# Filter spectra of a hybrid diffusion backbone on one Trainium2 core: stacked fp32r features, mirrored taps folded into sums and differences, one table for all slots

## The chip, the core and the metric

The kernel is one program on one core of a Trainium2 chip. The metric is device microseconds of that core from launch to end. Three timed runs of the kernel before gave 3165.01, 3173.91 and 3177.1 us; their median, 3173.91 us, is the time before.

The core's engines run side by side, each through its own queue in order: PE (matrix products), DVE (VectorE), ACT (ScalarE), POOL (GpSimd), and SP, which only issues DMAs. An engine waits for another through semaphores; whatever stands behind a waiting instruction on the same engine waits too.

## What is computed

The reference is a two-layer backbone over 2048 tokens of width 1024 (with 256 context tokens). Layer 0 is a pooling mixer beside attention with 6 query heads; layer 1 is a long-convolution mixer beside a Fourier mixer. The part that matters here are the filters of the long convolutions, which depend on no token: a small network gives 64 features for each of 2048 lags, a matrix turns them into taps for 768 channels, 2 orders and 2 directions, and the taps are damped and normalized.

```python
hdn = jnp.sin(fr * (hdn @ w2.astype(f32) + b2.astype(f32)))
h = (hdn @ w3.astype(f32)).reshape(L, HY_ORDER, 2, HY_WIDTH)
...
h = h * decay[:, None, None, :]
h = h / (jnp.sum(jnp.abs(h), axis=(0, 2), keepdims=True) + EPS)
zero = jnp.zeros((1, HY_ORDER, HY_WIDTH), f32)
return jnp.concatenate([h[:, :, 0], zero, h[:0:-1, :, 1]], axis=0)
...
kf = jnp.fft.rfft(kfull, n=2 * L, axis=0)
return jnp.fft.irfft(zf * kf[None], n=2 * L, axis=1)[:, :L]
```

The kernel stores `kf`, the spectra of 12 filters (6 blocks of 128 channels, 2 orders), and uses them in layer 1.

## The kernel before

The program has four stretches by the trace: layer 0's projections (0 to about 590 us), layer 0's attention (597 to 1755 us), a short stretch with layer 0's output projection, and layer 1 (from 2075 us on). **All of the change but a few instructions lies in the attention stretch**, because the spectra are computed in between the attention's matrix products.

*Attention.* There are 96 blocks of 128 queries (`blocks`). For each, PE computes five tiles of scores `S` in three products each (L306 to L308, fp32r in two parts), DVE takes maxima `mx` (L1295), ACT the exponentials into `pb` (L1306), PE transposes `pb` into `pt` (L1317), ACT and DVE split it into two parts `ph` and `pl` (L300, L303), and PE multiplies these with the values into `o` (L1329 to L1333). `S` and `pt` share six PSUM banks. The order of all this is written out by hand in the four strings of `BLOCK`: `S`, `M`, `E`, `T`, `V`, `D`, `N` and `Z` stand for the steps, a capital `F` calls `fill()`, which takes the filters' generator one `yield` further, and a `p` takes the generator `weights()` (called `prep`) one `yield` further. Two blocks hold five `F`, six `p`, and at every eighth pair one more fill (`f`).

*Filters.* `filters()` (L1116) runs over 12 units. A unit takes eight groups `grp` of four slots (a slot holds the 128 lags of one residue modulo 16); a group takes two `yield`s and the last one two more, so that a unit takes 18 fills. In a group, PE makes four products of 64 features by 128 channels in fp32 into `hacc` (L1173); DVE multiplies by the damping into `ht` (L1174), makes negated copies `hn` of half of it (L1175), sums absolute values (L1178) and adds them to `rd` (L1181); PE takes the first factor of the 2048-lag transform with a table of its own for each slot, `fdft`, eight fp32 products into `fa` (L1200, L1201); ACT copies `fa` to the slots of `fX` (L1203). The PSUM pool of `hacc` and `fa` has one bank, which they take in turns. The last group also forms the norm (`smacc`).

Once the eight groups of a unit are there, the second factor, a 16-point transform over the slots, runs on POOL: `fft16` returns 44 POOL operations for 64 channels, twice a unit, and `some(FFT_N)`, called after most `yield`s, gives POOL the next six of them, then stores the finished tile to DRAM (`spec`, L1134) `FFT_LATE` calls later.

*Weights.* Beside this, `weights()` prepares later weights in pieces. For 23 pieces of layer 1's input projection: load `wraw`, cast it to `wodd` on ACT (L1381), subtract on POOL (L1383), two `p` later store `wodd`. For 32 pieces of the output projections a product by the gate on POOL (L1403) stands between load and cast. There is one buffer of `wodd`.

So POOL's queue holds transforms and weights in the order in which the program gives them, ACT's holds exponentials, splits, copies of `fa` and casts of `wodd`, and SP's all loads and stores.

Of the kernel before, what the change touches and what calls it, by code (L numbers as in the profile page):

```python
# [40 lines left out]

BLOCK = [
# [15 lines left out]
def constants():  # L58
    """Tables that depend on the shapes alone."""
# [30 lines left out]
    sel = [[2 * q + 1, (2 * q + 2) % 16, 15 - 2 * q, 14 - 2 * q] for q in range(8)]  # L90
    out["decay"] = np.stack([dec[:, :, q, :] for q in sel], 1)
# [26 lines left out]
def sbc(ap, n):  # L118
    """[p, f] -> [p, n, f], the same f for each n."""
    return ap.unsqueeze(1).to_broadcast([ap.shape[0], n, ap.shape[1]])  # L120


def lbc(ap, n):
    """[p, f] -> [p, f, n], each element n times."""
    return ap.unsqueeze(2).to_broadcast([ap.shape[0], ap.shape[1], n])


def fft16(v, X, T, inv, s=None):
    """16-point transforms over the slots of X[p, re/im, 16, C]; T is of the same shape.

    Forward takes slot 4a+b and leaves index k'+4k'' in slot 4k'+k''; inverse undoes it,
    without the factor 1/16. The operations come as a list, each with its us. With s, that engine does the products by constants, beforehand.
    """
# [6 lines left out]
    def at(A, start, *dims):  # L140
        """slots of A, as (stride, count) from start on"""
# [14 lines left out]
    def stt(out, in0, scalar, op, in1):  # L156
        """in0 already has its factor where s does the products, but for the sign"""
# [28 lines left out]
    def tan(n, *dims):  # L186
        """the slots from n on, times the tangent"""
# [16 lines left out]
    # the second four: slots k * e + b * o for b; 11 and 14 have the other sign  # L204
# [35 lines left out]
def tile_net(ctx, tc, i, k, out, keep=None):  # L240
# [33 lines left out]
    def y1_part(kk):  # L274
        """the place of gated channels of layer 1"""
# [6 lines left out]
    hdd = dram("hdd", (8, 64, 4, P))  # L282
# [30 lines left out]
    class Lane:  # L313
        """pieces for one engine, each of so many us, the next one at least so many later, or after an event"""
# [30 lines left out]
    class Jobs:  # L345
        """the order in which work is given to the engines: matrix products in front, the rest when they are that far"""
# [37 lines left out]
        def until(self, done):  # L384
            """let time pass until done()"""
# [15 lines left out]
    def load_wout(sp, wp, w, kks, dst, gb, wait=4.0, eng=sy, ve=v):  # L401
        """output projection times the gate, in two parts, one tile of rows at a time"""
# [21 lines left out]
    def load_gate(wp, n):  # L424
        """the gate of layer n, the same in every partition"""
# [4 lines left out]
    def rstd_steps(sp, ss, n, tag, scale):  # L430
        """ss [p, n] sums of squares -> 1 / sqrt(ss * scale + eps), with a Newton step after the square root"""
# [13 lines left out]
    def normed_steps(sp, xs):  # L445
        """each slab [p, D] of xs -> each row over its root mean square, in place"""
# [13 lines left out]
    def modulated_steps(sp, pp, xs, gs, sh, emit, lo_eng):  # L460
        """transposed, scaled and shifted, in two parts: emit(m) gives their places"""
# [12 lines left out]
    LASTE, LASTR, GATE2, FOLD1, HALF, SUM0, SUM1, ADDF, FEW, LASTW, IN_C, FFT_N, FFT_LATE, HL, DR, DE, EW0, EW1, SPLIT, SUMMED, QSEL, CV0, CV1, CV2, CV3, COL, NW0, NW1, FIRST_Z, MORE, X0_SQ, X0_STEP, TRAIL, C_EARLY, A_TURN, A_SLOW, A_AHEAD, A_W, A_PACE, LAG0, FOLD, WAIT, AHEAD, LAG, APART, LOW, W_LOAD, W_HIGH, W_LOW, ADDED, SLOW = 0, 0.5, 5, 6, 1.5, 0.2, 1.5, 3, 9, 3.5, 25, 6, 4, 3, 4, 4, 8.0, 2.5, 15, 0.5, 1, 14, 12, 8, 15, 5, 24, 0, 20.0, 8, [7, 7, 11, 11], (0, 0, 0, 0, 2, 2, 2, 2), 11, 1, 2.5, 0.25, 3.5, 4, 1.05, 7, 2, 6.0, 2.5, 5, 5, 2, 6, 6, 4, 8, 1.02  # L474
    # tokens in the order n2 * 128 + n1 for token 16 * n1 + n2
# [8 lines left out]
    def load_columns(raw, gi, kk, half, eng=sy):  # L484
        """128 rows of half of the columns of a group"""
# [1886 lines left out]
```

## Time and profile before

| what | value |
|---|---|
| median of three runs | 3173.91 us (3165.01 to 3177.1) |
| span of the profiled execution | 3162.6 us |
| its time around the span | not in the profile; the fastest timed run is 2.4 us above the span |
| attention stretch | 597 to 1755 us |
| filters' products in it (`hacc`, `fa`) | from 611 to 1651 us |
| granted TensorE clock in it | 1.00 from 659 us on |
| PE busy over the span | 2996.1 us (95%) |

The profile is read here by stretches: busy time of an engine in a stretch of known work, then the rows of single operations by their shape, then the waits. Matmul records overlap their neighbours, so what a matmul costs its queue is the distance from its start to the next one's, not its length.

### The profile page before, as it was taken

The page shows a single profiled execution, that of the slowest core. Times are in us where ns is not written, and L with a number is a line of the kernel's source. Part 1 is how long each engine was busy: PE and PEld are TensorE (multiplying, and loading weights), DVE is VectorE, ACT ScalarE, POOL GpSimd, SP SyncE. Part 2 cuts the span into 40 slices and gives each one's busy share as a digit, 9 for nine tenths or more (in the row PEclk, how much of TensorE's full clock was granted, in tenths as well). Part 3 has the DMA queues.
Part 4 walks back from the last instruction along what each step waited for, and adds up shares of the span by engine and source line. Part 5 has one row for each costly group of instructions (what it writes and reads, how often), then busy time and mean ns, then how long its engine had stood idle before and what let it go on. Part 6 is the DMA issues. An engine that isn't in the chain of part 4 may idle for free. (4 is left out here: it accounts for less than half of the span.)

```text
span 3162.6 us, 49927 instructions
## 1 busy us (share of the span) xinstructions
PE 2996.1 (95%) x18121; PEld 2589.2 (82%) x18121; DVE 2183.2 (69%) x4124; ACT 1329.8 (42%) x3130; POOL 1215.5 (38%) x1595
## 2 busy tenths in 40 slices
PE   8999999799999999999999999999989999988799
PEld 4888888699999998999898778777878787874587
DVE  4775437477777777777776443377789797978556
ACT  4444545355555555555556332322323232232123
POOL 3122223027888887878886344001010100101110
PEclk9999999899999999999999999999999999999899
DMA  6466345534444445444443777678899989976875
GB/s 223 157 202 202 125 132 162 182 107 127 121 140 132 128 127 169 121 125 133 117 115 117 250 261 256 242 258 283 275 290 288 293 282 314 275 260 167 233 210 176
DMA packets 425393, 614.72 MB, mean 194 GB/s; under 512 B 140278, under 2 KB 278200, under 8 KB 416698
## 3 DMA queue, kind: packets, MB, share of 16 engines
q1 hardware_dynamic: 399994, 528.43, 51.0%
q0 software_dynamic: 25152, 83.10, 11.2%
q8 instruction: 143, 2.34, 0.3%
q14 instruction: 104, 0.85, 0.1%
HBM read 388.60 MB, written 187.18 MB: 182 GB/s over the span
## 5 line engine op out<-in xcount | busy, mean ns | idle before, releaser
L303 DVE TENSOR_TENSOR pl<-pt,ph 128x512 fp32r<-128x512 f32 (+1 forms) x480 | 299.8, 633 | 137.1 <-ACT ph L300 136.1
L151 DVE TENSOR_TENSOR gB<-gB 128x256 f32<-128x256 f32 (+3 forms) x442 | 351.6, 845 | 51.2 <-ACT gB L1879 47.3
L300 ACT CAST ph<-pt 128x512 fp32r<-128x512 f32 (+1 forms) x480 | 253.5, 556 | 244.7 <-PE pt L1317 242.3
L306 PE MATMUL dacc<-dh,dw 128*128 128x512 f32 x768 | 312.2, 407 | 40.2 <-DMA dh<-h1T 39.5
L1306 ACT ACTIVATE pb<-S,mx 128x512 f32<-128x512 f32 (+1 forms) x480 | 309.7, 656 | 82.7 <-DVE mx L1298 59.4
L307 PE MATMUL dacc<-dh,dw 128*128 128x512 f32 x768 | 304.7, 397 | 0.0
L308 PE MATMUL dacc<-dh,dw 128*128 128x512 f32 x768 | 304.6, 397 | 0.0
L1295 DVE TENSOR_REDUCE mx<-S 128x1 f32<-128x512 f32 (+1 forms) x480 | 279.9, 629 | 18.6 <-DMA kh<-kT0h 14.0
L303 POOL TENSOR_TENSOR wl<-raw,wh 128x256 fp32r<-128x256 f32 x160 | 135.6, 880 | 368.6 <-ACT wh L300 356.7
L1317 PE MATMUL pt<-ident,pb 128*128 128x128 f32 x1728 | 248.0, 275 | 11.2 <-ACT pb L1306 10.9
L151 POOL TENSOR_TENSOR fX<-fT 128x128 f32<-128x128 f32 (+2 forms) x336 | 246.7, 757 | 4.9
L1329 PE MATMUL o<-ph,vh 128*128 128x256 f32 x864 | 233.0, 301 | 1.4 <-ACT ph L300 1.2
L151 POOL TENSOR_TENSOR fT<-fX 128x1024 f32<-128x1024 f32 (+1 forms) x192 | 202.6, 1081 | 49.0 <-ACT fX L1203 44.6
L1317 PEld LDWEIGHTS pt<-ident,pb 128*128 128x128 f32 x1728 | 197.2, 141 | 28.2 <-ACT pb L1306 14.8
L1330 PE MATMUL o<-ph,vl 128*128 128x256 f32 x864 | 216.5, 282 | 1.5 <-DMA vl<-vl 1.5
L306 PEld LDWEIGHTS dacc<-dh,dw 128*128 128x128 f32 x768 | 147.9, 193 | 78.2 <-DMA dh<-h1T 46.7
L306 PE MATMUL S<-kh,qh 128*128 128x512 f32 (+1 forms) x480 | 196.9, 410 | 9.9 <-DMA kl<-kT0l 8.2
L306 PE MATMUL acc<-wh,hh 128*128 128x256 f32 x672 | 197.2, 293 | 3.5 <-ACT qraw L969 2.4
L308 PE MATMUL acc<-wh,hl 128*128 128x256 f32 x672 | 193.1, 287 | 1.2 <-DVE hl L303 0.9
L307 PE MATMUL acc<-wl,hh 128*128 128x256 f32 x672 | 192.8, 287 | 0.9 <-POOL wl L303 0.8
L307 PE MATMUL S<-kl,qh 128*128 128x512 f32 (+1 forms) x480 | 180.4, 376 | 1.1 <-DMA kl<-kT0l 1.0
L308 PE MATMUL S<-kh,ql 128*128 128x512 f32 (+1 forms) x480 | 180.4, 376 | 0.0
(473 smaller groups left out, 7776.5 us busy)
## 6 DMA issues: line engine op xcount, KB each, us to landing
dh<-h1T SPq DMA_DIRECT2D x172, 512.0 KB
dec<-cst_decay_dram SPq DMA_DIRECT2D x96, 256.0 KB
spec<-fX SPq DMA_DIRECT2D x24, 1024.0 KB
dw<-wi SPq DMA_DIRECT2D x48, 512.0 KB
gK<-spec SPq DMA_DIRECT2D x48, 512.0 KB
raw<-in_ev_w_in_dram SPq DMA_DIRECT2D x160, 128.0 KB
u<-dev SPq DMA_DIRECT2D x70, 256.0 KB
cu<-u POOLq DMA_DIRECT2D x17, 1024.0 KB, 8.3
```

What stands on the lines that cost most here:

```text
L151: put(out, lambda: v.tensor_tensor(out=out, in0=in0, in1=in1, op=op))
L300: s.copy(hi, src)
L303: lo_eng.tensor_sub(lo, src, hi.bitcast(F32))
L306: pe.matmul(acc, ah, bh, start=first, stop=False)
L307: pe.matmul(acc, ah, bl, start=False, stop=False)
L308: pe.matmul(acc, al, bh, start=False, stop=last)
L1295: v.tensor_reduce(out=B["mx"][:, c : c + 1], in_=S[:, :n], axis=AX.X, op=ALU.max)
L1306: s.activation(B["pb"][:, c * 512 : c * 512 + n], B["S"][c][:, :n], AF.Exp, bias=B["mx"][:, 5:6], accum_out=B["sm"][:, c : c + 1])
L1317: pe.transpose(pt[:, t, :], B["pb"][:, (4 * c + t) * P : (4 * c + t + 1) * P], ident)
L1329: pe.matmul(gr["o"], vh[:, a, :], ph[:, t, :], start=a == 0, stop=False)
L1330: pe.matmul(gr["o"], vl[:, a, :], ph[:, t, :], start=False, stop=False)
```

## The change

`w3` and the features are each split into an fp32r part and a rest. The two parts of the features are stacked on the 128 partitions (`fhd`, loaded once for all units), so that one product of 128 rows sums both; two such products (with the two parts of the weights) give a slot for both directions, 256 columns wide. A group is now a pair of mirrored slots (n, 16 - n), the last one the slots 0 and 8. DVE forms sum and difference (`sd`) of mirrored taps, so that one cosine and one sine table, 128 by 128 each and the same for all slots, do the first factor in two products of 256 columns; what differs between slots is a rotation by a known angle per frequency (`ftw`), done by ACT (`fU`, a product) and DVE (three operations that write `fX`). Absolute values go to ACT (`fab`), their sum to DVE (`rd`). `fX` holds all 128 channels of a unit, in two buffers; one transform of 128 channels takes the place of two of 64, and `FFT_N` goes from 6 to 5. Damping is loaded once for both directions. In layer 0's projections, the network's result is split and stored to `hdd` by four DMAs instead of ten.

```diff
-    sel = [[2 * q + 1, (2 * q + 2) % 16, 15 - 2 * q, 14 - 2 * q] for q in range(8)]
-    out["decay"] = np.stack([dec[:, :, q, :] for q in sel], 1)
+    out["decay"] = np.stack([dec[:, :, list(q), :] for q in PAIRS], 1)
...
+            s.copy(hd1.bitcast(F32R), hd2)
+            v.tensor_sub(hd2.bitcast(F32R), hd2, hd1)
...
+        def split_w3(u):
+            raw, skr = got[u]
+            w = sp.tile([P, 2, 3, P], F32R, tag="w3s", name="w3s", bufs=2)
+            for to, of in ((slice(0, 2), slice(0, 2)), (slice(2, 3), slice(0, 1))):
+                s.copy(w[:, 0, to], raw[:, of])
+                v.tensor_sub(w[:, 1, to], raw[:, of], w[:, 0, to].bitcast(F32))
+            got[u] = w, skr
+
+        mv(hd, hdd)
         fetch(0, 0)
+        fetch_w3(0)
         yield
-        sy.dma_start(dft, k["dft"])
+        sy.dma_start(dft, k["fdft"])
+        sy.dma_start(tw, k["turn"])
+        split_w3(0)
         yield
...
-                    acc = psum.tile([P, 4, P], F32, tag=tag, name="hacc")
-                    for q, n in enumerate((a0, a1, N2 - a0, (N2 - a1) % N2)):
-                        pe.matmul(acc[:, q, :], hd[:, q, :], w3[:, q // 2, :], start=True, stop=True)
-                    v.tensor_mul(ht, acc, dec)
-                    v.scalar_tensor_tensor(out=hn, in0=acc[:, 2:4, :], scalar=-1.0, in1=dec[:, 2:4, :], op0=ALU.mult, op1=ALU.mult)
+                acc = psum.tile([P, 2, 2, P], F32, tag=tag, name="hacc")
+                for q, t in enumerate((n, m)):
+                    to = slice(0, 2) if last or not q else slice(1, 3)
+                    for x in range(2):
+                        pe.matmul(acc[:, q].rearrange("p a b -> p (a b)"), hd[:, t, :], w3[:, x, to].rearrange("p a b -> p (a b)"),
+                                  start=x == 0, stop=x == 1)
+                v.tensor_mul(ht, acc, dec.unsqueeze(2).to_broadcast([P, 2, 2, P]))
+                if not last:
+                    v.tensor_add(sd[:, 0], ht[:, 0], ht[:, 1])
+                    v.tensor_sub(sd[:, 1], ht[:, 0], ht[:, 1])
+                ab = sp.tile([P, 2, 2, P], F32, tag="U", name="fab", bufs=2) if grp else rd
+                s.activation(ab, ht, AF.Abs)
...
-                    v.tensor_reduce(out=rd[:, min(grp, 1), :], in_=ht.rearrange("p a b -> p b a"), axis=AX.X, op=ALU.add,
-                                    apply_absolute_value=True)
-                    if grp:
-                        v.tensor_add(rd[:, 0, :], rd[:, 0, :], rd[:, 1, :])
+                if grp:
+                    v.tensor_add(rd, rd, ab)
...
-                            pe.matmul(fa[:, r, q, :], dft[:, n, r, :], ht[:, q, :], start=True, stop=False)
-                            pe.matmul(fa[:, r, q, :], dft[:, b, r, :], hn[:, q, :] if r else ht[:, 2 + q, :], start=False, stop=True)
-                    for x in range(2):
-                        s.copy(Xs[x][:, :, da, :], fa[:, :, :, x * 64 : x * 64 + 64])
-                    if grp == 7:
-                        for x in range(2):
-                            T = sp.tile([P, 2, N2, 64], F32, tag="T", name="fT")
-                            ops += [fn for fn, _ in fft16(g, Xs[x], T, False, g)]
+                        pe.matmul(fa[:, r].rearrange("p a b -> p (a b)"), dft[:, r], sd[:, r].rearrange("p a b -> p (a b)"), start=True, stop=True)
+                if last:
+                    s.copy(X[:, :, 0:9:8, :], fa)
+                    T = sp.tile([P, 2, N2, P], F32, tag="T", name="fT")
+                    ops += [fn for fn, _ in fft16(g, X, T, False, g)]
+                    ops.append((specd[j][o], X))
+                else:
+                    c, sn, ms = (tw[:, grp, x : x + 1] for x in range(3))
+                    U = sp.tile([P, 2, 2, P], F32, tag="U", name="fU", bufs=2)
+                    s.mul(U, fa, c)
+                    v.scalar_tensor_tensor(out=X[:, 0, n : m + 1 : m - n], in0=fa[:, 1], scalar=sn, in1=U[:, 0], op0=ALU.mult, op1=ALU.add)
+                    v.scalar_tensor_tensor(out=X[:, 1, n], in0=fa[:, 0, 0], scalar=ms, in1=U[:, 1, 0], op0=ALU.mult, op1=ALU.add)
+                    v.scalar_tensor_tensor(out=X[:, 1, m], in0=fa[:, 0, 1], scalar=sn, in1=U[:, 1, 1], op0=ALU.mult, op1=ALU.subtract)
```

The `BLOCK` strings and `weights()` stay as they are, so fills and `p` stand where they stood; what stands in them is new. The lines of the changed program lie some 6 to 34 lower in its own file. Three places of the program's order show what moved.

First PE's queue, the last products of scores before a fill, the fill with the products `fa`, and the first value products behind it; before:

```order
L306 MATMUL S<-kh_6865,qh 128x256
L307 MATMUL S<-kl_6866,qh 128x256
L308 MATMUL S<-kh_6865,ql 128x256
L1200 MATMUL fa<-ht,fdft 128x128
L1201 MATMUL fa<-ht,fdft 128x128
L1200 MATMUL fa<-ht,fdft 128x128
L1201 MATMUL fa<-hn,fdft 128x128
L1200 MATMUL fa<-ht,fdft 128x128
L1201 MATMUL fa<-ht,fdft 128x128
L1200 MATMUL fa<-ht,fdft 128x128
L1201 MATMUL fa<-hn,fdft 128x128
L1329 MATMUL o<-ph,vh_6892 128x256
```

and the same place now:

```order
L312 MATMUL S<-kh_6862,qh 128x256
L313 MATMUL S<-kl_6863,qh 128x256
L314 MATMUL S<-kh_6862,ql 128x256
L1230 MATMUL fa<-sd,fdft 128x256 x2
L1363 MATMUL o<-ph,vh_6891 128x256
```

Eight products of 128 columns have become two of 256; nothing around them moved.

Second DVE's queue over one group (the maxima of a block, the group's first fill, a split `pl` of the attention, the second fill); before:

```order
L1298 TENSOR_REDUCE mx<-mx 128x1
L1174 TENSOR_TENSOR ht<-hacc,dec 128x512
L1175 SCALAR_TENSOR_TENSOR hn<-hacc,dec 128x256
L303 TENSOR_TENSOR pl<-pt,ph 128x4x128
L1178 TENSOR_REDUCE rd<-ht 128x128
L1181 TENSOR_TENSOR rd<-rd 128x128
L303 TENSOR_TENSOR pl<-pt,ph 128x4x128
```

and now:

```order
L1332 TENSOR_REDUCE mx<-mx 128x1
L1195 TENSOR_TENSOR ht<-hacc,dec 128x512
L1197 TENSOR_TENSOR sd<-ht 128x256
L1198 TENSOR_TENSOR sd<-ht 128x256
L309 TENSOR_TENSOR pl<-pt,ph 128x4x128
L1204 TENSOR_TENSOR rd<-rd,fab 128x512
L1240 SCALAR_TENSOR_TENSOR fX<-fa,ftw,fU 128x2x128
L1241 SCALAR_TENSOR_TENSOR fX<-fa,ftw,fU 128x128
L1242 SCALAR_TENSOR_TENSOR fX<-fa,ftw,fU 128x128
L309 TENSOR_TENSOR pl<-pt,ph 128x4x128
```

The fill with `fa` now ends in three DVE operations that wait for `fU` of ACT, which waits for `fa` of PE; three operations instead of one read two tiles of SBUF (`sd` twice, `rd`).

Third POOL's queue at the start of a transform, in the changed program (L157 and L190 are operations of `fft16`, L1417 and L1437 the subtraction and the gate's product of `weights()`):

```order
L157 TENSOR_TENSOR fT<-fX 128x2x1024 x2
L157 TENSOR_TENSOR fX<-fT 128x2x512 x3
L1417 TENSOR_TENSOR wodd<-wraw,wodd 128x512
L157 TENSOR_TENSOR fX<-fT 128x2x512
L157 TENSOR_TENSOR fT<-fX 128x2x2x128 x2
L190 TENSOR_SCALAR fT<-fX 128x512 x2
L157 TENSOR_TENSOR fT<-fT,fX 128x128
L157 TENSOR_TENSOR fT<-fX,fT 128x128
L157 TENSOR_TENSOR fT<-fT,fX 128x2x128 x2
L157 TENSOR_TENSOR fT<-fT,fX 128x128
L1437 TENSOR_TENSOR wraw<-wraw,wgb 128x512
```

The gate's product stands behind 15 operations of the transform here; in the kernel before, such products stood behind as many operations of half the size.

More of the change, by code (lines that the diff above doesn't have):

```diff
@@ L40 @@
 EARLY, LATE = (0, 1, 2, 6, 7), (3, 4, 5)
+PAIRS = [(n, N2 - n) for n in range(1, 8)] + [(0, 8)]
 BLOCK = [
@@ L89, in constants @@
     dec = dec.reshape(128, 16, NCH, P).transpose(2, 0, 1, 3)
-    sel = [[2 * q + 1, (2 * q + 2) % 16, 15 - 2 * q, 14 - 2 * q] for q in range(8)]
-    out["decay"] = np.stack([dec[:, :, q, :] for q in sel], 1)
+    out["decay"] = np.stack([dec[:, :, list(q), :] for q in PAIRS], 1)
+    ang = 2 * np.pi * (k1[None, :] + 0.5) * (n1[:, None] + 0.5) / 256
+    ang0 = 2 * np.pi * (k1[None, :] + 0.5) * n1[:, None] / 256
+    out["fdft"] = np.stack([np.cos(ang), -np.sin(ang), np.cos(ang0), -np.sin(ang0)], 1)
+    ang = 2 * np.pi * (k1[:, None] + 0.5) * (np.arange(1, 8, dtype=f64)[None, :] - 8) / 4096
+    out["turn"] = np.stack([np.cos(ang), np.sin(ang), -np.sin(ang)], 2)
     d = np.arange(256, dtype=f64)
@@ L281, in tile_net @@
     wevd, wod = ([dram(f"w{x}{kk}", (P, 2, D)) for kk in range(KD)] for x in "eo")
-    hdd = dram("hdd", (8, 64, 4, P))
+    hdd = dram("hdd", (P, N2, P))
     fnd = dram("fn", (P, 2, 2, 256))
@@ L707, in tile_net @@
             v.scalar_tensor_tensor(out=gsc[2], in0=modc[:, 8:16], scalar=1.0, in1=gn, op0=ALU.add, op1=ALU.mult)
-            hq = hdd.rearrange("q p x c -> p q x c")
-            for half in range(2):
-                h4 = hd2[half * 64 : half * 64 + 64].rearrange("p (a b) -> p a b", a=8)
-                up, dn = slice(4 * half, 4 * half + 4), slice(4 - 4 * half, 8 - 4 * half)
-                sy.dma_start(hq[:, up, 0, :], h4[:, 1::2, :])
-                sy.dma_start(hq[:, dn, 2, :], h4[:, 7::-2, :])
-                sy.dma_start(hq[:, dn, 3, :], h4[:, 6::-2, :])
-                if half:
-                    sy.dma_start(hq[:, 3:7, 1, :], h4[:, 0::2, :])
-                else:
-                    sy.dma_start(hq[:, 0:3, 1, :], h4[:, 2::2, :])
-                    sy.dma_start(hq[:, 7, 1, :], h4[:, 0, :])
+            s.copy(hd1.bitcast(F32R), hd2)
+            v.tensor_sub(hd2.bitcast(F32R), hd2, hd1)
+            for x, part in enumerate((hd1, hd2)):
+                for half in range(2):
+                    sy.dma_start(hdd[x * 64 : x * 64 + 64, 8 * half : 8 * half + 8, :],
+                                 part[half * 64 : half * 64 + 64].rearrange("p (a b) -> p a b", a=8))
         hp = pool(st, "a_h", 18)
@@ L1119, in filters @@
         sp = pool(st, "f_u", 1, side="right")
-        dft = fc.tile([P, N2, 2, P], F32, name="fdft")
+        dft = fc.tile([P, 4, P], F32, name="fdft")
+        tw = fc.tile([P, 7, 3], F32, name="ftw")
+        hd = fc.tile([P, N2, P], F32R, name="fhd")
         late, ops = [], []
```

91 lines of the change are left out of this document (47 added, 44 removed).

## The prediction

> **What bounds the kernel now.** The granted clock was 1.00 through the stretch in question, so I went straight to the busy times of three windows: the start of attention, its steady part with filters, and its end without them.
>
> ```profile
> span 3162.6 us, 49927 instructions
> 600.00:610.00 10.00, 6.97 (x18) 4.86 (x19) 2.61 (x5) 4.25 (x10) 0.00 (x0) 0.50 0.99 284
> 659.00:1648.00 989.00, 975.12 (x7188) 895.12 (x7187) 758.42 (x1540) 556.78 (x1513) 787.80 (x1052) 1.00 0.45 128
> 1717.00:1755.00 38.00, 36.07 (x252) 31.88 (x251) 26.72 (x57) 24.62 (x67) 1.11 (x2) 1.00 0.76 267
> ```
>
> Columns: stretch, length, busy PE, weight loads, DVE, ACT, POOL, then clock, DMA share and GB/s. In the 989 us with filters PE is busy 99%, DVE 77%, ACT 56%, POOL 80%. So PE sets the pace, and POOL is the next fullest. The waits of this stretch say how the others hang on PE:
>
> ```profile
> ACT ph L300 <- PE pt L1317: 209.1, 136, 4.3
> ACT fX L1203 <- PE fa L1201: 139.9, 71, 5.5
> POOL wodd L1383 <- ACT wodd L1381: 109.0, 17, 14.7
> DVE pl L303 <- ACT ph L300: 107.8, 228, 2.9
> ACT wodd L1381 <- POOL wraw L1403: 6.2, 4, 2.3
> PE pt L1317 <- ACT pb L1306: 4.5, 6, 0.8
> ```
>
> (us in total, times, longest.) ACT waits for PE, DVE for ACT, and PE for almost nobody. POOL waits for ACT's casts of weights far more than ACT for POOL's products: POOL is ahead of the program. The change shortens PE's work and touches this last relation.
>
> **PE.** What a product costs its queue is the distance to the next start, so I read four places of the timeline (start, length, count):
>
> ```profile
> 1102.37 1.16 PE L1173 MATMUL hacc<-w,hd 64*128 64x128 f32 x8
> 1103.45 0.87 PE L1317 MATMUL pt<-ident,pb 128*128 128x128 f32 x6
> ...
> 1107.43 0.38 PE L1200 MATMUL fa<-ht,fdft 128*128 128x128 f32 x2
> ...
> 1109.13 0.48 PE L306 MATMUL S<-kh,qh 128*128 128x512 f32 x1
> ...
> 1112.92 0.28 PE L1329 MATMUL o<-ph,vh 128*128 128x256 f32 x1
> 1113.04 0.28 PE L1330 MATMUL o<-ph,vl 128*128 128x256 f32 x1
> ...
> 2832.70 5.56 PE L2100 MATMUL hacc<-M,G 128*128 128x256 f32 x25
> ```
>
> A group cost 1.08 us for `hacc` (1103.45 - 1102.37) and 1.70 for `fa` (1109.13 - 1107.43), together 2.78; each fp32 product leaves two records. After, `hacc` is four fp32r products of 128 by 256, the shape of the value products: 4 x 0.12 = 0.48 us. `fa` is two fp32 products of 256 columns, four records; 25 such records in layer 1 took 5.56 us, so (5.56 - 0.38) / 24 = 0.216 each, 0.86 in all (the last group's four of 128 columns take the same). 1.34 instead of 2.78: **1.44 us a group, 138 us for 96 groups**, all in the queue that sets the pace. Against that saving stand the other queues.
>
> **Units and fills.** DVE's products `ht` count the groups of the same window:
>
> ```profile
> L1174 DVE TENSOR_TENSOR ht<-hacc,dec 128x512 f32<-128x512 f32 x91 | 62.5, 687 | 24.9 <-PE hacc L1173 24.9
> L1175 DVE SCALAR_TENSOR_TENSOR hn<-hacc,dec 128x256 f32<-128x256 f32 x91 | 37.8, 415 | 0.0
> L1178 DVE TENSOR_REDUCE rd<-ht 128x128 f32<-128x512 f32 x92 | 98.4, 1069 | 0.0
> L1181 DVE TENSOR_TENSOR rd<-rd 128x128 f32<-128x128 f32 x81 | 40.5, 499 | 2.8
> ```
>
> 989 / 91 = 10.87 us a group, 86.9 a unit of eight. With PE alone it would be 86.9 - 8 x 1.44 = 75.4, and a fill (18 a unit) 4.2 us.
>
> **DVE.** Before, a group took 0.69 + 0.42 + 1.07 + 0.50 = 2.68 us. After: `ht` 0.69, sum and difference 2 x 0.42 (128x256, as `hn`), `rd` 0.69 (128x512, as `ht`), three that write `fX`, 0.42 and two of 128 columns at 0.29 (the shortest L1181, below): 3.2. With a split of weights, 0.7 a unit, about 4.5 us more a unit, 54 in all. DVE goes from 77% to about 758 + 11.4 x 4.5 = 810 of (989 - 131): 94%. I take nothing for it: its idle time before was waiting for PE and ACT, and its extra work fills that. Uncovered, it is 54 us at most.
>
> **ACT.** The two copies of `fa`, 0.38 each, become a product of 512 columns and an absolute value of 512. The nearest rows are a copy of that shape, 589 ns in layer 1, and an exponential of it, 696:
>
> ```profile
> L1522 ACT COPY dev<-dacc 128x512 f32<-128x512 f32 x64 | 37.5, 589 | 292.1 <-PE dacc L308 258.9 <-issue 29.6
> L1306 ACT ACTIVATE pb<-S,mx 128x512 f32<-128x512 f32 x384 | 265.7, 696 | 82.7 <-DVE mx L1298 59.4 <-DVE sc_n L1188 23.1
> ```
>
> That is 1.2 to 1.4 us instead of 0.76, about 0.5 more a group on an engine at 56%: nothing.
>
> **POOL, and what it holds up.** Here one transform of 64 channels starts and the next follows it:
>
> ```profile
> 1127.81 4.74 POOL L151 TENSOR_TENSOR fT<-fX 128x1024 f32<-128x1024 f32 x2 [5.54 <-ACT fX L1203]
> 1132.63 5.00 POOL L151 TENSOR_TENSOR fX<-fT 128x512 f32<-128x512 f32 x4
> ...
> 1153.23 1.72 POOL L151 TENSOR_TENSOR fX<-fT 128x128 f32<-128x128 f32 x4
> ...
> 1163.63 4.73 POOL L151 TENSOR_TENSOR fT<-fX 128x1024 f32<-128x1024 f32 x2
> ```
>
> 35.8 us, of which three operations on weights took 1.29 each: 31.9 for the 44 operations. 512 columns take 1.25 and 1024 take 2.37, so doubling a size adds what it had, less a fixed 0.19 (by the smaller shapes too). A transform of 128 channels is 2 x 31.9 - 44 x 0.19 = 55.4 us, against 63.8 for two of the old. POOL's total falls. But its **pace against the program** changes: before, 44 operations were handed out six a fill, over 7.3 fills of 4.8 us = 35 us for 32 us of work. Now they are handed out five a fill, over 8.8 fills of 4.2 = 37 us, for 55 us of work. From each unit's end POOL falls up to 18 us behind the program, and the weights' operations stand between the transform's. ACT's cast is in ACT's queue one `p` (six in 21 us, 3.5 us) behind POOL's product, and ACT waits there.
>
> How this looks can be seen once before:
>
> ```profile
> 1623.35 1.29 POOL L1403 TENSOR_TENSOR wraw<-wraw,wgb 128x512 f32<-128x512 f32 x1
> ...
> 1619.75 0.59 ACT L300 CAST ph<-pt 128x512 fp32r<-128x512 f32 x1 [0.48 <-PE pt L1317]
> 1624.67 0.62 ACT L1381 CAST wodd<-wraw 128x512 fp32r<-128x512 f32 x1 [4.34 <-DMA spec<-fX]
> ```
>
> The cast starts as the product ends (1624.64); the page names a DMA, but POOL came last. ACT stood 4.34 us, and PE lost nothing. So PE can do without ACT for some 4.5 us, and what goes beyond it, it loses.
>
> For the place shown in the change, the product is 15 operations in, 27 us of transform and 2.6 of weights: done 29.6 us after the start. The cast is 3.5 fills and a `p` behind, less the 1.5 us that POOL starts after that fill: 4.2 x 3.5 + 3.5 - 1.5 = 16.7. ACT waits 13 us. For a product 30 operations in (by the timeline 1153.23 - 1127.81 - 2.6 = 22.8 us for the first 28, about 23.7 for 30, 41.8 at double size, with weights 46): cast at 4.2 x 6.5 + 2 = 29.3, 16 us. A later wait is shorter by what an earlier one held PE up, so the longest counts. Counting the matmuls of the changed order up to each cast gives 12 to 16, mean 14, for the eight units in which gates' products stand; the same count for the kernel before gives four waits of up to 1.3 us, near the 6.2 us in four and the one of 4.3 above.
>
> To this comes **what DVE and POOL take from each other**. L1181 is short alone and long beside POOL:
>
> ```profile
> L1181 DVE TENSOR_TENSOR rd<-rd x84: 291/300/2026, 628.8 to 1643.6; 128x128 f32<-128x128 f32 x84
> ...
> 818.07 4.77 POOL L151 TENSOR_TENSOR fT<-fX 128x1024 f32<-128x1024 f32 x2
> ...
> 818.75 1.84 DVE L1181 TENSOR_TENSOR rd<-rd 128x128 f32<-128x128 f32 x1
> ```
>
> At 818.75 it lasted until POOL's first operation (half of the 4.77 us) was through. The change makes three such operations a group where there was one, and POOL's longest twice as long. POOL in turn waits while DVE reads: at most the three durations, 1.5 us a group, by the 4.77 us here (4.74 where DVE did nothing of the kind) next to nothing; I take 0.8, in five groups 4 us a transform. By the Trainium skill, page "SBUF — State Buffer", section "Who interferes with whom", a VectorE instruction with two inputs in SBUF and a GpSimd instruction that reads SBUF exclude each other for the whole instruction. The trace agrees: 1.84 us for what takes 0.29 alone. By that rule the sum below holds; without it the bursts would cost 11 x 4 = 44 us less.
>
> So a burst costs PE 14 + 4 - 4.5 = 13.5 us: **8 x 13.5 = 108 us**. In three earlier units (of the first phase, no gate) the cast waits instead for the one `wodd` buffer, whose store stands behind POOL's subtraction: 15 operations in, 29 us, landed 4 later, against a cast three `p` behind the subtraction, 4.2 x 3.5 - 1.5 + 10.5 = 23.7; a wait of 9, later in the burst up to 13, I take 11: 11 + 4 - 4.5 = 10.5, **32 us**. Bounds for a burst: nothing (PE rides through it) and 20 us (nothing rides).
>
> **The start.** Splitting the first weights now stands ahead of the first maxima on DVE, and its load behind the keys' and 1 MB of features: at the 284 GB/s above 3.7 us, and some more for damping and weights. In exchange the 2 MB table goes, for which PE waited (3.7 us, the first `fa`):
>
> ```profile
> PE fa L1200 <- DMA fdft<-cst_dft_dram: 3.7, 1, 3.7
> ```
>
> I take +4, bounds 0 and 8. The two split operations in the projections are a 1024-column ACT and DVE operation each, some 1.2 us beside PE's work: nothing, 2.4 if uncovered. Per-group loads shrink (features gone, damping halved) at a DMA share of 0.45: nothing. The single PSUM bank now stays taken until ACT's product and DVE's three are through, some 0.7 + 1.0 us after `fa`; between the closest fills stand 2.2 us of products: nothing, 1 us per pair of blocks (40 us) if DVE is late.
>
> **Sum.** -138 + 108 + 32 + 4 = +6 on a span of 3162.6. The median of the runs is 11.3 above this span, so about **3180**, no change to speak of: POOL takes PE's place during two thirds of each unit and gives the saving back.
>
> **Rivals.** *PE rides through the bursts*: ACT's wait reaches PE only in part, as no wait of ACT in this stretch was over 5.5 us, so none this long was seen. Then a burst costs some 2 us: -138 + 22 + 4 = -112, 3062. For it: POOL's work in all is less. Against: exponentials and splits stand behind the cast, and six PSUM banks last for a few us. That **the change doesn't do what it says** belongs here: were the fp32r products no faster than the old (0.27 each), PE would save 0.84 a group, 81 us, and the bursts, which POOL times, would cost some 5 us less each: again near the sum. *DVE becomes the bound*: after `ht`, sum and difference each wait for one operation of POOL, up to 4.6 us at a transform's start, and `fa` waits for them in PE's queue. It decides if these waits come on top of POOL's, where `fa` follows `ht` by one fill (4.2 us) and 1.5 + 4.6 + 2.3 us are needed: 4 to 5 us a burst, 50 in all, 3230. Against: while ACT stands at POOL, PE stands too, so both waits mostly overlap.
>
> **How the numbers follow.** The forecast has 0.60; its own range, with 4 us either way a burst (11 bursts), is 3130 to 3230. Rival one has 0.25, rival two 0.15. What a measurement of this kernel can tell from no change is about 0.5%, 3158 to 3190. Of the forecast I put 0.13 below, 0.25 within and 0.22 above; rival one is faster, rival two slower: 0.38, 0.25, 0.37. Eight in ten: 3085 to 3225, which takes in half of rival one and leaves out most of rival two.
>
> **What would show it.** In the changed profile ACT's casts of `wodd` wait 10 us and more for POOL, once or twice a unit; PE's idle time stands behind ACT; a unit takes 75 us where no burst stands (the first) and 85 to 90 elsewhere; `hacc` takes 0.48 us and `fa` 0.86; sum and difference last over 0.42 us beside POOL. Wrong would be units of 77 us throughout, or PE waiting for `sd`.

## The result and the profile after

The changed kernel took 3296.39 us in the median of 4 runs (3290.65 to 3301.93), the kernel before 3174.09 (3165.01 to 3177.1) beside it: ratio 1.0383, 95% interval 1.036 to 1.0406. The forecast was 3180 with a range up to 3225, so it was wrong by far more than a measurement's scatter.

The window of the filters' stretch as before the change, with the same columns (stretch, length, busy PE, weight loads, DVE, ACT, POOL, granted clock, DMA share, GB/s):

```profile
span 3300.1 us, 46570 instructions
659.00:1648.00 989.00, 826.54 (x5156) 712.44 (x5155) 829.48 (x1620) 545.16 (x1370) 667.72 (x514) 0.94 0.29 96
```

PE was busy 99% of these 989 us and is now busy 84%, as is DVE; no engine is full. The granted clock fell from 1.00 to 0.94. The maxima that close each block of attention tell where the time came from (nanoseconds of one, then first and last start):

```profile
L1298 DVE TENSOR_REDUCE mx<-mx x96: 157/158/161, 605.4 to 1754.4; 128x1 f32<-128x5 f32 x96
```

is the row of before, and

```profile
L1332 DVE TENSOR_REDUCE mx<-mx x96: 157/158/160, 617.1 to 1879.4; 128x1 f32<-128x5 f32 x96
```

that of after: attention's 95 blocks take 1262 us instead of 1149, 113 more; the start is 12 later. The waits of the stretch (us in total, times, longest) show who stands for whom now:

```profile
ACT wodd L1415 <- POOL wraw L1437: 45.5, 11, 9.4
ACT fab L1200 <- DVE ht L1195: 138.8, 67, 5.2
ACT ph L306 <- PE pt L1351: 69.5, 64, 3.4
PEld S L312 <- DVE pl L309: 67.0, 73, 6.5
PE fa L1230 <- DVE sd L1197: 26.4, 19, 3.8
PE fa L1230 <- DVE sd L1198: 18.1, 11, 3.9
PE hacc L1193 <- DVE fX L1242: 23.7, 24, 5.0
PE prb L1380 <- ACT bdg L1372: 16.7, 15, 2.7
```

Before, ACT waited 209 us for PE's transposes; now it is 70, and PE waits for DVE at four places. ACT's casts do wait for POOL, as I forecast, but only 45.5 us in all. DVE's rows say why it is late:

```profile
L1198 DVE TENSOR_TENSOR sd<-ht 128x256 f32<-128x256 f32 x72 | 90.6, 1258 | 0.0
L1197 DVE TENSOR_TENSOR sd<-ht 128x256 f32<-128x256 f32 x72 | 82.5, 1147 | 2.5
L1204 DVE TENSOR_TENSOR rd<-rd,fab 128x512 f32<-128x512 f32 x71 | 62.2, 876 | 0.0
L1195 DVE TENSOR_TENSOR ht<-hacc,dec 128x512 f32<-128x512 f32 x82 | 56.0, 683 | 6.3 <-PE hacc L1193 6.3
```

The sum and the difference take 1.15 and 1.26 us in the mean where the forecast's sum for DVE has 0.42; `ht`, one input of which is in PSUM, keeps its 0.68. Here is one transform's start in the timeline (start, length, in brackets the idle time before):

```profile
702.69 9.13 POOL L157 TENSOR_TENSOR fT<-fX 128x2048 f32<-128x2048 f32 x2 [6.66 <-ACT fX L1232]
...
708.21 3.89 DVE L1197 TENSOR_TENSOR sd<-ht 128x256 f32<-128x256 f32 x1
...
712.02 2.55 DVE L1198 TENSOR_TENSOR sd<-ht 128x256 f32<-128x256 f32 x1
714.50 0.41 DVE L309 TENSOR_TENSOR pl<-pt,ph 128x256 fp32r<-128x256 f32 x1
...
714.96 0.79 PE L312 MATMUL S<-kh,qh 128*128 128x512 f32 x1 [5.36 <-DVE pl L309]
```

The sum lasts until POOL's second operation is through (711.82), the difference until its next ones let it in; the split `pl` stands behind both in DVE's queue, and PE's scores, which need the bank that `pl` empties, stand 5.36 us. This looks like rival two. Whether it is the cause, the experiments had to show.

### The profile page after: what moved, and what is told of

It is laid out like the page before. It is cut to its first block, busy times and chain, and to the rows that moved or that the text cites. A ratio compares the mean times of both kernels' runs of the same rounds, so it can differ in the third digit from the quotient of the medians.

```text
span 3300.1 us, 46570 instructions
## 1 busy us (share of the span) xinstructions
PE 2936.3 (89%) x16633; PEld 2480.5 (75%) x16633; DVE 2353.9 (71%) x4413; ACT 1389.4 (42%) x3155; POOL 1158.3 (35%) x1067
## 5 line engine op out<-in xcount | busy, mean ns | idle before, releaser
L157 DVE TENSOR_TENSOR gB<-gB 128x256 f32<-128x256 f32 (+3 forms) x442 | 351.4, 844 | 50.1 <-ACT gB L1913 46.2
L1351 PE MATMUL pt<-ident,pb 128*128 128x128 f32 x1728 | 261.9, 282 | 40.4 <-ACT pb L1340 36.5
L312 PE MATMUL S<-kh,qh 128*128 128x512 f32 (+1 forms) x480 | 208.9, 435 | 61.7 <-DVE pl L309 32.7
L1351 PEld LDWEIGHTS pt<-ident,pb 128*128 128x128 f32 x1728 | 205.6, 145 | 66.9 <-ACT pb L1340 50.2
L1363 PE MATMUL o<-ph,vh 128*128 128x256 f32 x864 | 249.5, 317 | 0.2
L157 POOL TENSOR_TENSOR fX<-fT 128x256 f32<-128x256 f32 (+2 forms) x168 | 229.1, 1385 | 2.8
L1364 PE MATMUL o<-ph,vl 128*128 128x256 f32 x864 | 229.7, 295 | 0.0
L157 POOL TENSOR_TENSOR fT<-fX 128x512 f32<-128x512 f32 (+2 forms) x96 | 191.7, 2022 | 49.7 <-ACT fX L1232 47.8
L1417 POOL TENSOR_TENSOR wodd<-wraw,wodd 128x512 fp32r<-128x512 f32 x55 | 72.0, 1309 | 327.6 <-ACT wodd L1415 311.7
```

The lines of the kernel that those rows point to most:

```text
L157: put(out, lambda: v.tensor_tensor(out=out, in0=in0, in1=in1, op=op))
L312: pe.matmul(acc, ah, bh, start=first, stop=False)
L1351: pe.transpose(pt[:, t, :], B["pb"][:, (4 * c + t) * P : (4 * c + t + 1) * P], ident)
L1363: pe.matmul(gr["o"], vh[:, a, :], ph[:, t, :], start=a == 0, stop=False)
L1364: pe.matmul(gr["o"], vl[:, a, :], ph[:, t, :], start=False, stop=False)
L1417: g.tensor_sub(w[:, 1], raw, w[:, 0].bitcast(F32))
```

## The experiments

Theories on record: **L**, the lock (DVE's operations with two inputs in SBUF wait for POOL); **Q**, my forecast (ACT's casts stand behind POOL's products); **D**, DVE's load and the chain PE, DVE, ACT, DVE over one PSUM bank, whatever POOL does. Later came **S** (L and Q are two ways into one delay, and either one suffices), **R** (POOL costs time by a third way) and three forms of D. The kernels of a group, two to ten executions of each, ran on one chip beside the kernel before, whose median was 3169.9 to 3174.9 us in the five groups; so a difference of a few us between kernels of different groups says nothing.

| kernel | us | ratio to before, 95% |
|---|---|---|
| changed kernel | 3296.4 | 1.036 to 1.0406 |
| e1_psum_in | 3275.4 | 1.0295 to 1.0359 |
| e2_no_transform | 3175.0 | 0.9987 to 1.0011 |
| e3_four | 3279.5 | 1.0298 to 1.0381 |
| e4_sums_on_pe | 3275.8 | 1.029 to 1.0366 |
| e6_psum_no_weight_ops | 3182.9 | 1.0022 to 1.0055 |
| e7_no_weight_ops | 3251.7 | 1.0234 to 1.0294 |
| e8_no_magnitudes | 3081.8 | 0.9699 to 0.9756 |
| e9_sums_pe_product_ahead | 3233.3 | 1.0171 to 1.024 |
| e10_no_transform_abs_later | 3135.2 | 0.9826 to 0.9925 |
| e11_abs_later | 3272.4 | 1.0269 to 1.0348 |
| e12_pe_ahead_abs_later | 3218.6 | 1.0091 to 1.0185 |
| e13_pe_ahead_abs_later_diag | 3215.7 | 1.0045 to 1.0214 |
| e14_pe_two_buffers | 3211.7 | 1.0077 to 1.0172 |
| e15_dve_two_buffers | 3211.0 | 1.008 to 1.0165 |
| e16_no_transform_no_rd | 3102.6 | 0.9741 to 0.9821 |
| e17_three_raw | 3213.3 | 1.0099 to 1.0143 |
| e18_three_raw_four | 3168.2 | 0.9969 to 1.0004 |
| e19_dve_no_weight_ops | 3165.9 | 0.9952 to 0.9992 |

**What do the transforms cost, and is it the lock?** e1 takes the lock from sum and difference (they read an undamped tap from PSUM, so its spectra are not the reference's), e4 moves them to PE, e2 leaves the transforms out, e3 hands out four of their operations a fill.

```diff
 e1
-                    v.tensor_add(sd[:, 0], ht[:, 0], ht[:, 1])
-                    v.tensor_sub(sd[:, 1], ht[:, 0], ht[:, 1])
+                    v.tensor_add(sd[:, 0], acc[:, 0], ht[:, 1])
+                    v.tensor_sub(sd[:, 1], acc[:, 0], ht[:, 1])
 e2
-                    ops += [fn for fn, _ in fft16(g, X, T, False, g)]
+                    g.tensor_copy(T[:, 0, 0, 0:1], X[:, 0, 0, 0:1])
+                    ops += [lambda: None] * 44
 e3 (in the line of numbers)
-FFT_N = 5
+FFT_N = 4
 e4 (no tensor_add, no tensor_sub; a fifth table, +sin)
+                        for q in range(2):
+                            pe.matmul(fa[:, r]..., dft[:, 4 if r and q else r], ht[:, q]..., start=q == 0, stop=q == 1)
```

> Sum and difference of mirrored taps take their first input from PSUM (undamped, so the spectra are not the reference's); number, length and place of all operations stay. Theory L (what DVE's operations with two SBUF inputs wait for POOL's transforms makes DVE the bound): their 99.8 and 89.5 us for 80 and 79 fall to 0.42 us each, DVE is 120 us lighter in the stretch, and the time falls by 70 to 120 us, to 3175 to 3225. Theory Q (ACT's casts behind POOL's products, as forecast): no change, 3285 to 3310, or longer waits of the casts. Theory D (DVE's load and the chain PE-DVE-ACT-DVE over one PSUM bank, whatever POOL does): no change within 15 us.

> The 16-point transforms on POOL are left out (spectra are stored without their second factor); calls, stores, fills stay. L and Q both: all of POOL's part goes, time 3296 - 150 or more, 3100 to 3150. D: units run as the first unit of the changed kernel did without transforms beside it, 12.2 us a block instead of 13.3, so about 80 us less, 3200 to 3230; if neither chain nor load mattered, PE alone would give about 3045.

> FFT_N 4 instead of 5: POOL's products of weights stand behind fewer operations of the transform. Q: the casts' waits (46 us measured in the stretch) nearly go, and the time falls by 20 to 40 us. L: the same operations of DVE meet the same operations of POOL, within 12 us of 3296. D: within 12 us.

> PE forms sum and difference in its accumulation (four products of 256 columns with three tables instead of two), DVE's two operations go: PE +0.86 us a group, 2.2 instead of 1.34 against 2.78 before; DVE -0.84 us a group without the waits. L: the waits go with them, time 3296 - 120 to 180 = 3115 to 3175, at or under the kernel before. D: DVE's load falls too and the chain from hacc to fa is shorter; 3150 to 3220. Q: nothing gained, PE's 73 us more hide the casts' waits, 3270 to 3330.

Without the transforms the kernel is as fast as before (e2): they cost 121 us, and PE's saving is lost without them too. The 3175 lies between the ranges, under D's 3200 and over the 3150 of L and Q. The lock's going brought 21 us (e1), not the 70 and more that L wanted; e4 brought as much, with some 72 us more work on PE (84 groups of 0.86 us) and less on DVE. e3's 17 us lie between Q's 20 and the 12 of the others. The row of the sum (nanoseconds shortest, median, longest) and ACT's waits in e1:

```profile
L1197 DVE TENSOR_TENSOR sd<-hacc,ht x79: 424/425/426, 667.3 to 1726.9; 128x256 f32<-128x256 f32 x79
```

```profile
ACT wodd L1415 <- POOL wraw L1437: 78.8, 13, 14.3
ACT wodd L1415 <- DMA wraw<-in_od_w_in_dram: 29.2, 9, 8.5
```

The lock is gone (424 to 426 ns for every one of 79), and in its place ACT stands 108 us at its casts where it stood 46. The longest of them, in e1's timeline:

```profile
1586.44 1.26 POOL L1437 TENSOR_TENSOR wraw<-wraw,wgb 128x512 f32<-128x512 f32 x1
...
1587.73 0.62 ACT L1415 CAST wodd<-wraw 128x512 fp32r<-128x512 f32 x1 [14.35 <-POOL wraw L1437]
...
1588.97 0.48 DVE L1240 SCALAR_TENSOR_TENSOR fX<-fa,ftw,fU 128x256 f32<-128x256 f32 x1 [10.56 <-ACT fU L1239]
...
1590.12 1.19 PE L1193 MATMUL hacc<-w3s,fhd 128*128 128x256 f32 x4 [11.56 <-DVE fX L1242]
```

This is the burst of my forecast, at the 14 us that it took for the mean; it is the longest of e1's 13 waits for POOL's product, and the next has 11.1. The cast starts as POOL's product ends, `fU` stands behind the cast, `fX` behind `fU`, and PE's next `hacc` behind the bank. In the changed kernel it shows little. That DVE has already held everything up there is theory S, for the next group to test.

**Both away.** e6 and e7 leave out POOL's operations on weights, and with the waits for them the work itself, 98 of POOL's 668 us in the window of the changed kernel; e8 leaves out the magnitudes; e9 keeps everything and gives the product by the gate to POOL one tile earlier.

```diff
 e6 (on e1), e7 (on the changed kernel)
-                g.tensor_sub(w[:, 1], raw, w[:, 0].bitcast(F32))
-                mv(dst, w)
+                for x in range(2):
+                    mv(dst[:, x], w[:, 0])
...
-                        g.tensor_mul(raw, raw, gb)
 e8 (on e2)
-                s.activation(ab, ht, AF.Abs)
+                if not grp:
+                    s.activation(ab, ht, AF.Abs)
-                if grp:
-                    v.tensor_add(rd, rd, ab)
 e9 (on e4), in parts(raw, dst, ahead)
                 g.tensor_sub(w[:, 1], raw, w[:, 0].bitcast(F32))
+                if ahead:
+                    ahead()
```

> e1_psum_in with POOL's operations on weights left out too (the gate's product and the subtraction; the rounded half is stored in both places, so gates and low halves are missing in the output). Theory S (two waits for one delay: POOL's transforms hold up DVE by the shared input and, when that is gone, ACT by the casts behind POOL's products; each one alone costs almost what both do): with both out the transforms cost next to nothing, the time is that of e2_no_transform, 3165 to 3200. Theory R (the transforms cost time by a third way, the last two-input operation `rd`, the buffers of X or the stores): 3235 or more. Theory L alone (first theory: the lock is everything): as e1, about 3275.

> The changed kernel with only POOL's operations on weights left out (gate's product and subtraction), DVE's sum and difference as they are. Theory Q (my forecast: ACT's casts behind POOL's products are the cost of the bursts): about 3175. Theory S: the lock alone still costs nearly the whole, 3250 to 3290; POOL's own 60 us less work per transform window shortens it a little.

> e2_no_transform with the magnitudes left out too (ACT's absolute values and DVE's additions to `rd` in groups 1 to 7, 84 of each; the filters' norms are wrong then). It takes 0.77 us from DVE and 0.63 from ACT a group, 65 and 53 us in all. Theory D1 (DVE's and ACT's load eats PE's saving): 3100 to 3125. Theory D2 (the chain of waits over the one PSUM bank, PE to DVE to PE to ACT to DVE to PE, eats it; the magnitudes are not in that chain, only beside it): 3150 to 3175. If PE's saving came through fully it would be about 3050.

> e4_sums_on_pe, and the product by the gate for the next weights is given to POOL one tile ahead (four `p` before the cast instead of one); everything is computed. Theory S: both waits are gone but for the first product of a transform, 3185 to 3220. Theory R: 3260 or more. It beats the kernel before only if the chain of theory D is looser here, since PE saves only 0.7 us a group.

The lock alone away: 21 us. The weights alone away (e7): 45. Both away (e6): 113 of the 121 that the transforms cost, with POOL's transforms still running. (By the ratios to the kernel before beside each: 18, 38 and 110 of 122.) So S held, with e7 at the lower edge of its range, L and Q each fell as the only cause, and R has no place of any size in this group. e9, with everything computed, came 43 below e4, 13 above its range. e8 showed that what is left without POOL is not PE: 93 us for 65 of DVE's and 53 of ACT's work, more than either form of D had foreseen.

**Where PE's saving goes without POOL.** Without the transforms ACT still waits for `ht`: it is given the absolute value in the same fill as the product that makes its input, and all that stands behind it in ACT's queue waits too.

```profile
659.00:1648.00 989.00, 894.26 (x5824) 772.68 (x5824) 814.25 (x1832) 611.95 (x1545) 111.56 (x96) 0.98 0.32 107
```

```profile
ACT fab L1200 <- DVE ht L1195: 165.6, 78, 5.3
```

are the window and the wait of e2. e10 (on e2; like e8 and e16 it also lacks e2's 44 empty calls, so that the spectra are stored some 40 us earlier, which was not tried apart), e11 (on the changed kernel) and e12 (on e9) issue the absolute value one fill later; e13 also moves `D`.

```diff
-                s.activation(ab, ht, AF.Abs)
                 yield
+                s.activation(ab, ht, AF.Abs)
                 some(FFT_N)
 e13
-    "T0 p S0 S1 F S2 S3 S4 M T1 f p F D V3 V4 E1 N E3 T2 E0 T3 p E4 E2 F T4 Z",
+    "T0 p S0 S1 D F S2 S3 S4 M T1 f p F V3 V4 E1 N E3 T2 E0 T3 p E4 E2 F T4 Z",
```

> e2_no_transform with ACT's absolute values issued one fill later, where their input has long been there; ACT then does not stand at `ht` (165.6 us in 78 waits in the window 660 to 1700 of e2_no_transform). Same work on every engine. Theory D3 (without POOL, it is ACT standing in line at `ht`, with exponentials, casts and `bdg` behind it, that eats PE's saving): most of what leaving the magnitudes out brought (3175 to 3082), 3085 to 3115. Theory D1 (the load of DVE and ACT, 0.77 and 0.63 us a group, eats it): 3160 to 3175.

> The changed kernel with only the absolute values one fill later; everything is computed. DVE's sum and difference still share SBUF with POOL's transforms. Theory S with D3: the lock keeps its 120 us, ACT's stand at `ht` goes: 3200 to 3240. Theory D1: 3285 to 3300.

> e9_sums_pe_product_ahead (3233) with the absolute values one fill later; everything is computed. Theory D3: 3150 to 3180, PE's 0.7 us a group begin to show. Theory D1: 3225 to 3240.

> e12_pe_ahead_abs_later with the softmax's diagonals (`D`, two ACT operations) given out before the first fill of the even block instead of behind the third; everything is computed. PE stood 22.8 us at `prb` for them in the window 660 to 1700 of e9. If that wait is real and not replaced: 15 to 35 us below e12 (their waits times 96/74, and the clock after each); if ACT is merely late everywhere: as e12 within 8 us.

```profile
659.00:1648.00 989.00, 909.66 (x6105) 802.84 (x6104) 838.38 (x1897) 640.81 (x1621) 112.60 (x97) 0.99 0.35 115
```

```profile
ACT fab L1201 <- DVE ht L1195: 3.5, 2, 2.0
DVE rd L1204 <- ACT fab L1201: 26.6, 30, 1.5
```

These are the same of e10: the stand is gone and the time falls by 40 us, between D1 and D3. ACT is idle hardly less, 348 us of the 989 instead of 377: it now waits 270 us for transposes (`ph`) and maxima (`pb`), in e2 93. So it was not the standing that cost, but what stood behind it. DVE's additions to `rd` now wait for the later `fab`, the last row. With POOL beside it the same edit brought 24 (e11) and 15 (e12), below what D3 wanted. e13 brought nothing clear: PE's wait for `D`, 13.3 us in e12, is gone, but its transposes stand 26.1 us for exponentials instead of 15.2 (window 660 to 1700), and the time stays within its scatter of e12's.

**DVE's load, and a version that might keep the saving.** e16 leaves out only DVE's additions to `rd`. e14 and e15 compute everything: e14 is e12 with two buffers for `wodd`, one instead of two for `ht` and for `sd` to make room, and the first weights loaded first; e15 has the same on the change's own products, with the first tap written a second time in PSUM.

```diff
 e15
+                    v.tensor_mul(acc[:, 0], acc[:, 0], dec[:, 0:1, :].to_broadcast([P, 2, P]))
-                    v.tensor_add(sd[:, 0], ht[:, 0], ht[:, 1])
-                    v.tensor_sub(sd[:, 1], ht[:, 0], ht[:, 1])
+                    v.tensor_add(sd[:, 0], acc[:, 0], ht[:, 1])
+                    v.tensor_sub(sd[:, 1], acc[:, 0], ht[:, 1])
...
-                w = wp.tile([P, 2, 512], F32R, tag="w", name="wodd")
+                w = wp.tile([P, 2, 512], F32R, tag="w", name="wodd", bufs=2)
```

> e12_pe_ahead_abs_later (3219) with two buffers for a rounded weight (`wodd`; `ht` and `sd` have one each to make room) and the start in another order (first weights, then damping, then the features); everything is computed. In e12 ACT's casts still stood 70 us in the window 660 to 1700 for the stores that had to leave the one buffer. If that is the rest of Q, and the start gives back half of its 12 us: 3165 to 3195. If ACT's stand was covered: 3205 to 3220 (start alone).

> The changed kernel with the lock gone in another way: DVE writes the first tap's product a second time, in place in PSUM (0.42 us more a group), and sum and difference take it from there; PE's products stay as in the change. With the product ahead, two buffers for `wodd`, the absolute values later and the start as in e14; everything is computed. By S and D3: e6's 3183 less e10's 40 and the start's 6, plus 35 for DVE's added work if DVE counts in full (e8 against e10): 3135 to 3175. It beats the kernel before if DVE's added work is half covered. If theory R held after all (a third way by which transforms cost time): 3200 or more.

> e10_no_transform_abs_later (3135) with only DVE's 84 additions to `rd` left out, 0.78 us each (the norms are wrong); ACT's absolute values stay. Theory D1 for the rest (DVE's load counts in full, although DVE is busy only 85%): 65 us less, 3065 to 3080. If the rest lies in ACT's load: 3115 to 3130, and the absolute values are the other part of e8's 3082.

e16 fell 32 us below e10, between its two ranges, for 62 us of DVE's work (84 additions of 0.74 us in e10) and the stand at `fab` that goes with them: DVE's load counts by half at most. e14 gained 7, what the start was to give; so ACT's stand for stores had been covered, unless the single buffers took back what its end was worth. e15 missed: 3211, not 3175 or less, which is in R's range.

**The last 40 us.** e17 gives raw weights a third buffer (for the room, `fab` is written over `ht`, and `fU` has one buffer), e18 hands out four operations a fill on top, e19 is e15 without POOL's operations on weights.

```diff
 e17 (on e15)
-                return wp.tile([P, 512], F32, tag="raw", name="wraw", bufs=2)
+                return wp.tile([P, 512], F32, tag="raw", name="wraw", bufs=3)
...
-                ab = sp.tile([P, 2, 2, P], F32, tag="U", name="fab", bufs=2) if grp else rd
+                ab = (sp.tile([P, 2, 2, P], F32, tag="U", name="fab", bufs=1) if last else ht) if grp else rd
...
-                    U = sp.tile([P, 2, 2, P], F32, tag="U", name="fU", bufs=2)
+                    U = sp.tile([P, 2, 2, P], F32, tag="U", name="fU", bufs=1)
 e18 (on e17)
-FFT_N = 5
+FFT_N = 4
```

> e15_dve_two_buffers (3211) with three buffers for raw weights instead of two (the absolute values are written in place, and `fU` has one buffer, to make room); everything is computed. In e15 ACT's casts still stood 33 us in the window 660 to 1700 for loads that wait for POOL's subtraction two tiles back, up to 10 us at once, and scores stood up to 9.2 us behind them. If these stands are what is left of theory S: 3165 to 3190. If another way holds (theory R): 3205 or more.

> e17_three_raw with four of POOL's operations handed out a fill instead of five, so that POOL falls behind less and its operations on weights come sooner; everything is computed. If POOL's being late still costs: 10 to 20 us below e17 (e3 against the changed kernel: 17). If not: within 6 us of e17.

> e15_dve_two_buffers with POOL's operations on weights left out (gates and low halves are missing in the output): no wait of ACT for POOL is left, and of DVE's waits for POOL only that of `rd`, 0.27 us a group. Theory S: e10's 3135 less 6 for the start plus DVE's added work, 0.42 + 0.17 us a group at the half price that e16 gave (25): 3145 to 3165. Theory R: 3185 or more.

```profile
659.00:1648.00 989.00, 858.38 (x5567) 750.70 (x5566) 813.21 (x1830) 588.65 (x1479) 705.28 (x548) 0.96 0.30 101
```

```profile
ACT wodd L1416 <- DMA wraw<-in_od_w_in_dram: 34.9, 7, 8.5
ACT wodd L1416 <- POOL wraw L1455: 11.2, 6, 4.0
ACT wodd L1416 <- POOL wraw L1446: 8.0, 1, 8.0
```

are the window and ACT's waits of e17, where the third buffer, with what was given up for it, changed nothing (3213, in R's range again). In e18 POOL has fewer transform operations in front of each weight:

```profile
659.00:1648.00 989.00, 887.24 (x5861) 777.09 (x5860) 850.62 (x1917) 617.22 (x1553) 734.67 (x570) 0.98 0.32 107
```

```profile
ACT wodd L1416 <- DMA wraw<-in_od_w_in_dram: 11.8, 5, 4.8
ACT wodd L1416 <- POOL wraw L1446: 5.0, 1, 5.0
```

ACT's stands at the casts fall from 54 to 17 us, the time by 45, where 10 to 20 were expected. e19 came out at 3166, one us above S's range and far from R's 3185: the last 40 us were POOL's weights again. The same edit of one number was worth only 17 in the changed kernel (e3), by S because the lock stood for it there. e18 computes everything and is as fast as the kernel before (interval 0.9969 to 1.0004); no version that computes everything was faster.

## Why the prediction was wrong

**PE's saving: right in size.** By the distance to the next start, one group in the profile after:

```profile
705.21 0.71 PE L1193 MATMUL hacc<-w3s,fhd 128*128 128x256 f32 x4
705.76 0.38 PE L1351 MATMUL pt<-ident,pb 128*128 128x128 f32 x2
...
1065.41 1.03 PE L1230 MATMUL fa<-sd,fdft 128*128 128x256 f32 x4
1066.27 0.82 PE L1351 MATMUL pt<-ident,pb 128*128 128x128 f32 x6
```

0.55 and 0.86, together 1.41 (forecast 1.34): 1.37 saved a group, 132 us instead of 138.

**DVE "I take nothing", ACT "nothing", the single bank "nothing": the step that failed.** The argument was that DVE's idle time before was waiting for PE and ACT, so more work would fill it. e2 is that sum without POOL: it should have taken 3174 - 138 + 4 = 3040 and took 3175. Of these 135 us, 6 are PE's, and 6 the start's: e2's first maxima come at 615.6, 10 later than before, where I took 4. ACT's stand at `ht` cost 40 (e10 against e2), DVE's additions to `rd`, with their stand, 32 (e16 against e10). ACT's absolute values are some 20 more (e8 against e16, in two groups, whose intervals overlap). What is left, some 30, is not settled: the bank and the three `fX` were not tried apart, nor the granted clock, of which the forecast's sum says nothing and which was 0.98 in e2 and 0.94 in the changed kernel. DVE was never full (814 of 989 us in e2). Its work counted because it stands in line: a filter's operation delays the attention's operation behind it, and PE needs that one.

**POOL's bursts: 140 us forecast, 121 measured, by another door.** The size was about right, in part by luck, and the place mostly wrong. The forecast put all of it on ACT's casts, which waited 46 us for POOL in all, and used the lock only for the 4 us that POOL loses; in the changed kernel DVE pays it. Both doors lead to the same delay, as the forecast said in words of its second rival but did not price: shutting DVE's gave 21 us, shutting ACT's 45, both 113. Even by ACT's door alone (e1) the waits were shorter than worked out, 14.35 us once and 11.1 and less otherwise, where 14 was the mean; of the longest PE rode through 2.8 (14.35 less 11.56), not 4.5.

**The sum.** Of the +122 us, the terms taken as nothing ate what PE saved (e2 against before: +1), and the bursts gave the 121. The start's 12 in the changed profile (forecast 4, bounds 0 to 8) are among the first. With the first weights loaded first (e14, e15, e17 to e19) the first maxima came at 611 to 613 us, in the other runs at 612 to 622: the order accounts for a few us, and the rest was not followed up.

**The rivals.** "PE rides through the bursts" fell with e1. "DVE becomes the bound" had the right mechanism for the changed kernel, sum and difference behind POOL and `fa` behind them, at 50 us; it was given 0.15 because ACT's and DVE's waits were to overlap. They do overlap, which is why taking one away changes little; but it does not make them cheap.

**What was to show it.** `hacc` and `fa` did (0.55, 0.86), and sum and difference over 0.42 beside POOL (1.15 and 1.26). ACT's waits of 10 us and more did not (longest 9.4), nor units of 85 to 90: 82 groups in 989 us make 96.5 a unit. PE waiting for `sd`, named as the sign that the forecast is wrong, stands in the profile with 44.5 us.

## What to carry to other kernels

When the engine that sets the pace gets 12% less work, the order of the others' queues sets it next, at 80 to 85% busy: count the waits that each added operation puts in front of somebody else's, and give an operation out when its input is there, not when its input is asked for (for one line here 40 us without the transforms, 24 with them). A late worker with two customers has to be cut off from both before either is judged: 21 and 45 us apart were 113 together. The pace at which a side job is handed out belongs to the main loop's pace: after PE's work a fill had shrunk, five operations a fill were too many, and four were worth 17 us with the other wait left in and 45 without it.

## What the hardware showed beside it

An idle PE cost more than the idle time here. In the changed kernel PE stood 2.63 us for the one bank, and then (PE's rows, and the granted clock in the windows behind them):

```profile
1059.78 1.19 PE L1193 MATMUL hacc<-w3s,fhd 128*128 128x256 f32 x4 [2.63 <-DVE fX L1242]
1060.77 0.41 PE L1363 MATMUL o<-ph,vh 128*128 128x256 f32 x1
1060.99 0.41 PE L1364 MATMUL o<-ph,vl 128*128 128x256 f32 x1
...
1063.08 0.28 PE L1363 MATMUL o<-ph,vh 128*128 128x256 f32 x1
1063.20 0.28 PE L1364 MATMUL o<-ph,vl 128*128 128x256 f32 x1
```

```profile
1060.00:1062.40 2.40, 2.40 (x12) 2.40 (x13) 1.35 (x3) 0.60 (x2) 0.00 (x0) 0.50 0.22 82
1063.00:1066.00 3.00, 2.92 (x24) 2.63 (x23) 1.36 (x3) 2.48 (x8) 0.00 (x0) 1.00 0.00 0
```

The value products start 0.22 us apart at a clock of 0.50 and 0.12 apart at 1.00: some 2.7 us at half pace, over 1.3 us lost on top of the wait. The Trainium skill, page "TensorE: Matmul & The Clock Gate", section "Part 1: The HAM clock gate (the "warmup" mystery)", says that an idle window of about 3.4 us takes the clock to half and a busy one gives it back. The trace agrees on the half and on the way back; an idle time of 2.63 us was enough here. Over the stretch the clock of 0.94 is, as an estimate from the window's row, 6% of PE's 827 busy us, some 50 us. A count of the work says much the same: 82 groups at what one took PE before, less the saving (975.12 / 91 - 1.37 = 9.35 us), are 766 us, and PE was busy 827. This is part of what every wait above cost, and no run took it apart.

The lock showed its condition plainly: 128x256 with two inputs in SBUF took 424 to 4634 ns beside POOL,

```profile
L1197 DVE TENSOR_TENSOR sd<-ht x79: 424/809/4634, 668.5 to 1750.4; 128x256 f32<-128x256 f32 x79
```

and with one input in PSUM 424 to 426 (e1's row above), while POOL ran the same transforms. The Trainium skill, page "SBUF — State Buffer", section "Who interferes with whom", states both: two inputs in SBUF contend with a GpSimd instruction that reads SBUF; with at most one, and outside the 2-port perf modes, there is no contention. The trace agrees, with these two rows.
